# Other orders for the Strassen products of a two-layer encoder's MLP, with finer units of split weights

## The chip, the cores and the metric

One core of one Trainium2 chip runs the whole program. The metric is the device time of one execution in microseconds (us), the median of several runs. TensorE (PE in the profile) multiplies, VectorE (DVE), ScalarE (ACT) and GpSimd (POOL) do the element-wise work, SyncE (SP) issues the transfers; PSUM is the memory that TensorE accumulates in.

## The reference

An encoder of two layers on 544 tokens (512 of one sequence and 32 of another) of width 1024. Each layer adds two attention mixers, a cross-attention to 256 memory tokens and an MLP to the residual x. The change is in the MLP, and in what borders on it:

```
def rmsnorm(x, g):
    y = xf * lax.rsqrt(jnp.mean(jnp.square(xf), axis=-1, keepdims=True) + EPS)
    return y * g
...
    for l in range(DEPTH):
        x = x + mixers(rmsnorm(x, norm_mix[l]))
        x = x + cross_attention(rmsnorm(x, norm_cross[l]), mk, mv, w_xq[l], w_xo[l])
        hm = rmsnorm(x, norm_mlp[l])
        x = x + jnp.square(jax.nn.relu(hm @ w_up[l])) @ w_down[l]
    y = rmsnorm(x, norm_final)
```

Here w_up is 1024 x 4096 and w_down 4096 x 1024 in each layer, all in float32; the attention caches are outputs too.

## The kernel before

Activations lie transposed, features on the partitions, tokens along the free axis in two halves of 272. To keep float32's accuracy, each weight and activation is split into a high part (a cast by ScalarE to the short format fp32r) and a low part (a subtraction by VectorE, or by POOL in the attention), and a product is three matmuls: low x high, high x high, high x low (`mm3`).

The program is a list of steps with nominal costs (`then`), written in the order in which TensorE is to do them; a scheduler underneath may exchange neighbours that are ready. The order of each engine is fixed when the program is built, and an engine runs its own instructions strictly in that order.

The MLP (`mlp`, line 1405) goes through the 4096 hidden features in four groups per layer. A group has an *up stage*: eight blocks of 128 features (`dense`, 8 steps of 6 matmuls, 128x272 columns each, so 48), whose results `evac_up` brings out of PSUM, and from which `sums_up` and `rest_up` make the seven operands (B11, TA and so on) of a Strassen-Winograd scheme, again as high and low parts. Then comes the *down stage*: four *pairs* (two 128-feature blocks of the output each, `pair`, line 320). A pair loads its quarter of w_down with two transfers of 512 KB (L327), makes the weight sums S1 to S4 by four additions (`add`, L332), splits the seven weight operands in units (`split`, L342 on ScalarE and L343 on VectorE) and does seven products of 12 matmuls each (`product`, matmul on L358).

Three PSUM banks serve a pair: X and Z are the two halves of one tile (two such tiles exist, and the dense blocks use them too), W is another tile. The scheme's intermediate sums stay in the bank: after each product `evac_pair` (L1075, on VectorE) adds the bank as it then stands into one or two quarters of the residual X, and a later product goes on accumulating in the same bank. So the next product on a bank must wait until the addition after the one before has read it. `PRODUCTS` gives unit, operand and bank of the seven products; their banks in turn are X, Z, X, Z, X, W, X, pair after pair.

`UNITS` says which weight operands are split together: three units of two operands (1024 columns), which share a ring of two buffers (uh, ul), and one of one operand (512 columns), which takes a place in the ring of three (wh, wl) that the dense weights use as well. The table `todo` in `mlp` says before which product a load, an addition or a split is issued. In the last group of layer 0 each finished quarter is also prepared for the next layer's norm (`prep`: ScalarE's cast, VectorE's L401, ScalarE's square and POOL's sum L416), in the last of layer 1 for the final norm (`finish`, `final_sum`, `final_norm`), whose products by the norm's factor VectorE and POOL share by the table `OUT`. `next_block` says which dense weights are split during the last pair; `load_weights` issues their transfers (raw<-w_up, L238) on SP's queue, in which the transfers of w_down stand too.

## Time and profile before

| what | value |
|---|---|
| median of 3 runs | 1705.31 us (1704.8 to 1708.51) |
| profiled execution | 1705.88 us, span of its instructions 1704.1 us |
| mean granted TensorE clock | 0.993 of 2.4 GHz |
| TensorE busy | 1621.1 us, 12159 matmuls |
| VectorE busy | 1107.2 us |
| ScalarE busy | 794.6 us |
| POOL busy | 316.8 us |
| DMA | 157.22 MB, mean 92 GB/s |

The profile follows one execution. A row of a timeline gives the start and the duration of an instruction, engine, line, operation, the output and inputs by the program's names, and in brackets how long the engine had been idle and what it waited for. Matmuls overlap in the engine, so one is listed with 0.28 to 0.29 us although they start 0.12 to 0.13 us apart.

### The profile page before, as it was taken

The numbers are of one execution on the slowest core, as the hardware profiler recorded it, in microseconds if no ns is written. First come the engines' busy times: TensorE is split into PE (matmuls) and PEld (weight loads), VectorE is DVE, ScalarE is ACT, GpSimd is POOL, SyncE is SP. The second block draws the span as 40 slices with busy tenths as digits, with TensorE's granted clock in tenths as the row PEclk, the third lists the DMA queues.
The fourth block names the chain that finished last, engine by engine and source line by source line (L and its number), as shares of the span: only waits on it lengthen the run. The fifth ranks groups of instructions, "written<-read, shape, count | busy, mean of one in ns | idle before, by whom it ended". The sixth has DMA issues, their size and how long they took to land. (4 is left out here: it accounts for less than half of the span.)

```text
span 1704.1 us, 30118 instructions
## 1 busy us (share of the span) xinstructions
PE 1621.1 (95%) x12159; PEld 1516.3 (89%) x12159; DVE 1107.2 (65%) x2103; ACT 794.6 (47%) x1509; POOL 316.8 (19%) x297
## 2 busy tenths in 40 slices
PE   8899999999999999999889999999999999998995
PEld 7777889998999989899887778999999999898995
DVE  6956673456667677676777657535576676766765
ACT  6656664444443434334446646544444334243443
POOL 4514233321200000000244213333120000000003
PEclk9999999999999999999999999999999999999998
DMA  4322255223323222222123113642232222222211
GB/s 162 97 70 76 79 165 164 87 75 107 95 70 105 80 83 93 81 92 79 39 85 96 64 58 110 188 118 85 75 112 87 87 87 87 87 82 80 88 63 53
DMA packets 56395, 157.22 MB, mean 92 GB/s; under 512 B 6768, under 2 KB 16048, under 8 KB 56256
## 3 DMA queue, kind: packets, MB, share of 16 engines
q1 hardware_dynamic: 55984, 155.02, 29.2%
q8 instruction: 95, 1.56, 0.4%
q14 instruction: 44, 0.36, 0.1%
q10 hardware_dynamic: 272, 0.28, 0.0%
HBM read 143.49 MB, written 11.75 MB: 91 GB/s over the span
## 5 line engine op out<-in xcount | busy, mean ns | idle before, releaser
L289 PE MATMUL pd<-Ah,wl 128*128 128x272 f32 (+2 forms) x2032 | 458.9, 296 | 8.5 <-DVE wl L259 5.6
L289 PE MATMUL pd<-Ah,wh 128*128 128x272 f32 (+2 forms) x2032 | 441.5, 288 | 1.2 <-ACT Ah L400 1.2
L289 PE MATMUL pd<-Al,wh 128*128 128x272 f32 (+2 forms) x2032 | 440.4, 288 | 0.1
L256 ACT CAST wh<-raw 128x512 fp32r<-128x512 f32 (+1 forms) x362 | 222.0, 615 | 317.8 <-PE pd L289 244.7
L289 PEld LDWEIGHTS pd<-Ah,wl 128*128 128x128 f32 (+1 forms) x2032 | 327.9, 188 | 21.3 <-issue 9.6
L289 PEld LDWEIGHTS pd<-Ah,wh 128*128 128x128 f32 (+1 forms) x2032 | 327.1, 188 | 2.8 <-ACT Ah L400 2.2
L289 PEld LDWEIGHTS pd<-Al,wh 128*128 128x128 f32 (+1 forms) x2032 | 327.3, 188 | 0.3 <-DVE Al L401 0.3
L416 POOL TENSOR_TENSOR acc<-acc,sq 128x544 f32<-128x544 f32 x47 | 75.8, 1612 | 854.1 <-ACT sq L415 500.3
L259 DVE TENSOR_TENSOR wl<-raw,wh 128x512 fp32r<-128x512 f32 (+1 forms) x260 | 183.7, 707 | 50.8 <-ACT wh L256 50.3
L342 ACT CAST uh<-w 128x1024 fp32r<-128x1024 f32 x96 | 100.7, 1048 | 218.3 <-PE pd L358 214.9
L259 POOL TENSOR_TENSOR wl<-raw,wh 128x512 fp32r<-128x512 f32 (+1 forms) x102 | 133.0, 1304 | 338.0 <-ACT wh L256 229.6
L358 PE MATMUL pd<-Bh,ul 128*128 128x272 f32 x320 | 98.8, 309 | 38.6 <-DVE XG L1075 28.9
L1075 DVE TENSOR_TENSOR XG<-XG,pd 128x272 f32<-128x272 f32 x192 | 80.6, 434 | 78.5 <-PE pd L358 77.0
L343 DVE TENSOR_TENSOR ul<-w,uh 128x1024 fp32r<-128x1024 f32 x96 | 118.8, 1238 | 16.5 <-ACT uh L342 15.2
L289 PE MATMUL pd<-Bh,wl 128*128 128x272 f32 (+1 forms) x576 | 124.3, 294 | 1.2 <-DVE qr L718 0.7
L289 PE MATMUL pd<-Bh,wh 128*128 128x272 f32 (+1 forms) x576 | 121.2, 289 | 0.0
L289 PE MATMUL pd<-Bl,wh 128*128 128x272 f32 (+1 forms) x576 | 121.1, 289 | 0.0
L358 PEld LDWEIGHTS pd<-Bh,ul 128*128 128x128 f32 x320 | 60.6, 189 | 49.8 <-DVE XG L1075 34.5
L332 DVE TENSOR_TENSOR w<-w 128x512 f32<-128x512 f32 x128 | 92.4, 724 | 11.5 <-DMA w<-w_down 10.9
L289 PEld LDWEIGHTS pd<-Bh,wl 128*128 128x128 f32 x576 | 90.6, 188 | 3.8 <-issue 1.0
L358 PE MATMUL pd<-Th,ul 128*128 128x272 f32 x320 | 92.8, 290 | 0.0
L358 PE MATMUL pd<-Bl,uh 128*128 128x272 f32 x320 | 92.8, 290 | 0.0
(309 smaller groups left out, 3077.7 us busy)
## 6 DMA issues: line engine op xcount, KB each, us to landing
w<-w_down SPq DMA_DIRECT2D x64, 512.0 KB, 4.4
raw<-w_up SPq DMA_DIRECT2D x64, 512.0 KB, 3.5
raw<-w_in SPq DMA_DIRECT2D x28, 512.0 KB, 3.5
raw<-w_mk SPq DMA_DIRECT2D x16, 512.0 KB, 3.8
raw<-w_mv SPq DMA_DIRECT2D x16, 512.0 KB, 3.8
raw<-w_out SPq DMA_DIRECT2D x16, 512.0 KB, 3.6
raw<-w_xq SPq DMA_DIRECT2D x16, 512.0 KB, 3.6
raw<-w_xo SPq DMA_DIRECT2D x16, 512.0 KB, 3.6
```

The source lines that it names most:

```text
L256: nc.scalar.copy(h[:, :n], r)
L259: eng.tensor_tensor(lo[:, :n], r, h[:, :n].bitcast(F32), ALU.subtract)
L289: nc.tensor.matmul(o, w, a[:, c0:c1], start=start and n == 0, stop=stop and n == 2)
L332: self.nc.vector.tensor_tensor(w[:, o], w[:, a], w[:, b], ALU.add)
L342: self.nc.scalar.copy(h, r)
L343: self.nc.vector.tensor_tensor(lo, r, h.bitcast(F32), ALU.subtract)
L358: self.nc.tensor.matmul(st[bank], w[:, c], a, start=first and i == 0 and m == 0, stop=i == HP - 1 and m == 2, skip_group_check=True)
L416: nc.gpsimd.tensor_tensor(self.acc, self.acc, sq, ALU.add)
L1075: self.nc.vector.tensor_tensor(x, x, ps, op)
```

## The change

The seven products of a pair come in another sequence, with names (Q1, N5, N6, Q3, Q7, Q2, P4), and the table `GROUP` interleaves the pairs of a group (`LAST` does so for the last group of layer 1). W22 and W12 become units of their own, so that a pair has two units of 1024 and three of 512 columns. `plan` works out from `GROUP` and from the sizes of the two rings (`RINGS`) before which product a split, a load or an addition stands. All eight weight additions of a group's first two pairs move into its up stage (six before), and the first splits of pairs 0 and 1 too. The last product of a group, P4 of pair 3, runs inside the first block of the next group's up stage, after three of its eight steps (`resume`), with its split, its addition and the next load; for the last group of layer 0 that block is the first of layer 1. `AT` moves the norm and its use in layer 1's start, `final_norm` takes the rows of `OUT` by the order of the two halves, and the last sums of the final norm are made by halves for two pairs. Lines below the tables lie ten further down than before: 1075 becomes 1085, 358 becomes 368.

```diff
@@ -30,7 +30,7 @@
 
 AT = (dict(norm=1, take=(1.1, 2, 3), gate=3.5, sums=15, keys=24, rows=24, norm_cq=16, norm_ckv=22, split_ckv=27,
             rotary=25),
-      dict(norm=7, take=[13], gate=21, sums=42, keys=45, rows=51, norm_cq=38, norm_ckv=42, split_ckv=53, rotary=54))
+      dict(norm=10, take=[15], gate=21, sums=42, keys=45, rows=51, norm_cq=38, norm_ckv=42, split_ckv=53, rotary=54))
 
 POS = (dict(kr=1, v0=1, v1=4, qr0=2, qr1=2),
        dict(kr=1, v0=1, v1=3, qr0=2, qr1=2))
@@ -55,10 +55,20 @@
 W11, S1, W12, W22, S3, S2, S4 = range(7)
 W21 = S1
 
-UNITS = ((W11, 2), (S2, 2), (S3, 1), (W12, 2))
-
+UNITS = ((W11, 2), (S2, 2), (W12, 1), (S3, 1), (W22, 1))
+
+Q1, N5, N6, Q3, Q7, Q2, P4 = range(7)
 PRODUCTS = ((0, 0, B11, "X", True), (0, 1, TA, "Z", True), (1, 0, TB, "X", False), (1, 1, B22, "Z", False),
-            (2, 0, TC, "X", False), (3, 0, B21, "W", True), (3, 1, TD, "X", False))
+            (3, 0, TC, "X", False), (2, 0, B21, "W", True), (4, 0, TD, "X", False))
+
+GROUP = ((0, Q1), (0, N5), (1, Q1), (1, N5), (0, N6), (0, Q3), (0, Q2), (0, Q7), (1, N6), (1, Q3), (0, P4), (1, Q2),
+         (1, Q7), (2, Q1), (2, N5), (1, P4), (2, N6), (2, Q3), (2, Q2), (2, Q7), (3, Q1), (3, N5), (2, P4), (3, N6),
+         (3, Q3), (3, Q2), (3, Q7), (3, P4))
+
+LAST = GROUP[:18] + ((3, Q1), (2, Q7), (3, N5), (2, Q2), (3, N6), (3, Q3), (3, Q2), (3, Q7), (2, P4), (3, P4))
+
+RINGS = ((2, (0, 1), 4), (3, (2, 3, 4), 7))
+TAIL = 3
 HP = 4
 
 PAIRED = (0, 4, 1, 5, 2, 6, 3, 7)
@@ -1075,13 +1085,13 @@
         self.nc.vector.tensor_tensor(x, x, ps, op)
         if goff is None:
             return
-        if goff == G_FIN and i == HP - 1:
-            if n == 4:
+        if goff == G_FIN and i >= HP - 2:
+            if n == Q7:
                 self.finish(i, 1)
                 self.finish(m, 1)
-            elif n > 4:
+            elif n in (Q2, P4):
                 self.finish(m, 0)
-        elif n > 4:
+        elif n in (Q2, P4):
             if goff == G_FIN:
                 self.square(m)
                 self.nc.scalar.mul(self.X[:, m], self.X[:, m], self.g[:, goff + m:goff + m + 1])
@@ -1104,7 +1114,7 @@
         c = slice(j * HALF, (j + 1) * HALF)
         self.nc.tensor.matmul(ps, self.ones_r.bitcast(F32), self.acc[:, c], start=True, stop=False)
 
-    def final_norm(self, j):
+    def final_norm(self, j, n):
         nc = self.nc
         c = slice(j * HALF, (j + 1) * HALF)
         R = self.rp.tile([128, NT], F32, tag="r", name="R")
@@ -1112,7 +1122,7 @@
-        for b, eng in OUT[j]:
+        for b, eng in OUT[n]:
...
@@ -1293,12 +1303,13 @@
-            self.then([(0, lambda l=l: self.open_mixers(l))])
+            if l == 0:
+                self.then([(0, lambda: self.open_mixers(0))])
...
-            tkf = win(None, take[0], 96, **first)
+            tkf = win(None, take[0], 96, ahead=0)
...
@@ -1309,8 +1320,8 @@
                 first = [ckv] + f0
                 take = [lambda f=f, j=j: f(raw[j]) for j, f in enumerate(evac)]
             else:
-                first = [tkf] + cq + [ckv] + f0
                 take = [tkf.pop()[1]]
+                first = [self.resume(tkf, tail, len(self.order) - 7)] + cq + [ckv] + f0
             flat = [s for j in first for s in j]
             p = AT[l]
             assert p["norm"] <= p["take"][0] <= p["gate"] <= p["sums"] <= p["keys"] <= p["rows"]
@@ -1400,14 +1411,15 @@
                          for h in range(4)], t[3] + 8.4)
 
             goff = G_MIX + 8 if l == 0 else G_FIN
-            self.mlp(l, A, goff, bind, at, behind)
+            tail = self.mlp(l, A, goff, bind, at, behind)
 
     def mlp(self, l, A, goff, bind, at, behind):
         groups = []
         for grp in range(4):
-            up = [self.dense(io["w_up"][l, 8 * grp + j], 128, *A, bind(self.evac_up, j), ahead=int(n < 7))
-                  for n, j in enumerate(PAIRED)]
+            up = [self.dense(io["w_up"][l, 8 * grp + j], 128, *A, bind(self.evac_up, j),
+                             ahead=int(n < 7 and (n or not grp))) for n, j in enumerate(PAIRED)]
             down = [self.pair(io["w_down"][l, grp, i], lambda n, ps, i=i, g=goff if grp == 3 else None:
                               self.evac_pair(i, g, n, ps)) for i in range(HP)]
             groups.append((up, down))
@@ -1417,23 +1429,16 @@
         def do(f, *a):
             self.then([(0, lambda: f(*a))])
 
...
+        def call(n, what, *a):
             if n < len(pairs):
+                pairs[n][what](*a)
+
+        do(call, 0, "load")
+        do(call, 1, "load")
+        tail = None
         for grp, (up, down) in enumerate(groups):
             p0 = HP * grp
+            end = l == L - 1 and grp == 3
             if grp == 0:
                 up[0], up[1] = behind(up[0], up[1], self.norm, *NORM[l]["mlp"])
             for n in range(8):
@@ -1443,72 +1448,84 @@
                     up[n + 1] = at(up[n + 1], 5 + late, self.rest_up)
                     up[n + 1] = at(up[n + 1], 2 + late, self.sums_up, j)
 
-                if n >= 2:
-                    up[n] = at(up[n], 8, adds, p0 + (n >= 6), *((0, 1, 2, 3, 0, 1)[n - 2:n - 1]))
+                if n:
+                    up[n] = at(up[n], 8, call, p0 + n // 5, "add", (n - 1) % 4)
                 if n == 7:
-                    up[n] = at(up[n], 1, split, p0, 0)
-                    up[n] = at(up[n], 5, split, p0, 1)
+                    up[n] = at(up[n], 9, call, p0 + 1, "add", 3)
+                    up[n] = at(up[n], 1, call, p0, "split", 0)
+                    up[n] = at(up[n], 5, call, p0 + 1, "split", 0)
+            if grp:
+                up[0] = self.resume(up[0], tail, after - 8 * (4 - grp))
             for s in up:
                 self.then(s)
...
+            prods = LAST if end else GROUP
+            todo = self.plan(prods, p0, call)
+            q1 = len(prods) - (0 if end else 1)
+            todo[0].insert(0, (self.sums_up, 7))
+            todo[1].insert(0, (self.rest_up,))
+            if not end:
+                nxt = after - 8 * (3 - grp)
+
+                late = [(call, p0 + HP - 1, "split", 4), (call, p0 + HP + 1, "load")]
+                todo = {q: [f for f in fs if f not in late] for q, fs in todo.items()}
+                todo[q1 - 3].append((self.split_weights, nxt, 1))
+                todo[q1 - 1].extend(late)
             for q, (i, n) in enumerate(prods):
-                p = p0 + i
-                if q == 0:
-                    do(self.sums_up, 7)
-                if q == 1:
-                    do(self.rest_up)
-                for f, *a in todo.get((i, n), []):
+                for f, *a in todo.get(q, []):
                     do(f, *a)
-                if l == L - 1 and grp == 3 and q == len(prods) - 1:
-                    do(self.final_sum, 1)
-                self.then([(1.5, lambda p=p, n=n: pairs[p]["product"](n))])
-                if before:
-                    do(pairs[before[0]]["evac"], before[1])
-                before = p, n
-            do(pairs[before[0]]["evac"], before[1])
+                if q == q1:
+                    break
+                self.then([(1.5, lambda p=p0 + i, n=n: pairs[p]["product"](n))])
+                if q:
+                    i, n = prods[q - 1]
+                    do(pairs[p0 + i]["evac"], n)
+            i, n = prods[q1 - 1]
+            if end:
+                self.pn = {}
+                do(self.final_sum, 1)
+            do(pairs[p0 + i]["evac"], n)
+            tail = [(1.5, lambda p=p0 + HP - 1: pairs[p]["product"](P4))], [
+                (0, lambda p=p0 + HP - 1: pairs[p]["evac"](P4))]
         if l == L - 1:
-            self.pn = {}
-            do(self.final_norm, 1)
+            do(self.final_norm, 1, 0)
             do(self.final_sum, 0)
-            do(self.final_norm, 0)
-        do(self.close_mlp)
-
...
+    def resume(self, steps, tail, idx):
+
+        product, evac = tail
+        w = [[(0, lambda a=a: self.split_weights(*a))] for a in ((idx,), (idx + 1, 1), (idx + 1,))]
+        return (w[0] + steps[:TAIL] + product + steps[TAIL:TAIL + 1] + evac + steps[TAIL + 1:TAIL + 3] + w[1] +
+                steps[TAIL + 3:8] + w[2] + steps[8:])
+
+    def plan(self, prods, p0, call):
+
+        use, free, todo = {}, {}, {}
+        for q, (i, n) in enumerate(prods):
+            use.setdefault((i, PRODUCTS[n][0]), []).append(q)
+
+        def when(q, i, *a):
+            todo.setdefault(q, []).append((call, p0 + i) + a)
+
+        for rank, (ring, units, ahead) in enumerate(RINGS):
+            order = sorted((k for k in use if k[1] in units), key=lambda k: use[k][0])
+            for n, (i, u) in enumerate(order):
+                q = max(use[order[n - ring]][-1] + 1 if n >= ring else 0, use[i, u][0] - ahead)
+                assert q < use[i, u][0] or (i, u) == (0, 0)
+                free[i] = max(free.get(i, 0), q)
+                if u or i > 1:
+                    todo.setdefault(q + 0.5, []).append((call, p0 + i, "split", u))
+        for i in range(HP):
+            when(free[i] + 0.7, i + 2, "load")
+        for i in (2, 3):
+            a, b = [use[i, u][0] - 5 for u in (0, 1)]
+            for k, q in enumerate((a - 1, a, b - 1, b)):
+                when(max(q, free[i - 2] + 3), i, "add", k)
+        return {q: [f for k in sorted(todo) if int(k) == q for f in todo[k]] for q in range(len(prods))}
 
     def run(self):
         nc, io = self.nc, self.io
```

VectorE at the start of a group's down stage (the first of layer 0). L1131 and L1148 to L1154 bring out the last up block and form its sums, L1139 the low parts of the operands, L1075 adds a bank into the residual XG; pd_6060 is the tile with banks X and Z of pair 0, pw_6144 its bank W. Before:

```order
L1139 TENSOR_TENSOR Tl3_5109<-G_5110,Th3_5107 128x272
L1139 TENSOR_TENSOR Tl3_5109<-G_5110,Th3_5107 128x544 x2
L1075 TENSOR_TENSOR XG_85<-XG_85,pd_6060 128x272
L343 TENSOR_TENSOR ul_6094<-w_5501,uh_6093 128x1024
L1075 TENSOR_TENSOR XG_85<-XG_85,pd_6060 128x272 x2
L332 TENSOR_TENSOR w_6097<-w_6097 128x512
L343 TENSOR_TENSOR ul_6128<-w_5504,uh_6127 128x1024
L1075 TENSOR_TENSOR XG_85<-XG_85,pd_6060 128x272 x2
L1075 TENSOR_TENSOR XG_85<-XG_85,pw_6144 128x272
```

In the changed kernel (ten lines further down), pd_6070 is the tile of pair 0 and pd_6102 that of pair 1:

```order
L1149 TENSOR_TENSOR Tl3_5109<-G_5110,Th3_5107 128x272
L1149 TENSOR_TENSOR Tl3_5109<-G_5110,Th3_5107 128x544 x2
L1085 TENSOR_TENSOR XG_85<-XG_85,pd_6070 128x272
L353 TENSOR_TENSOR ul_6099<-w_5501,uh_6098 128x1024
L1085 TENSOR_TENSOR XG_85<-XG_85,pd_6070 128x272
L1085 TENSOR_TENSOR XG_85<-XG_85,pd_6102 128x272 x2
L353 TENSOR_TENSOR ul_6137<-w_5504,uh_6136 128x1024
L342 TENSOR_TENSOR w_6120<-w_6120 128x512
L1085 TENSOR_TENSOR XG_85<-XG_85,pd_6070 128x272 x2
L1085 TENSOR_TENSOR XG_85<-XG_85,pw_6166 128x272
```

After the first two additions of pair 0 come two of pair 1, and only then the third and fourth of pair 0; the split in front of them is of pair 1's weights.

TensorE where a group ends and the next up stage begins; pd_6407 and pd_6414 hold banks X and Z of pair 3, pd_6522 and pd_6525 are the first up block's. Before, the last product stood in front of most of the block (single steps were pulled ahead of it):

```order
L289 MATMUL pd_6522<-Al_87,wh_6458 128x272 x2
L289 MATMUL pd_6522<-Ah_86,wl_6459 128x272 x2
L289 MATMUL pd_6522<-Ah_86,wh_6458 128x272 x2
L358 MATMUL pd_6407<-Bh_88,ul_6439 128x272
L358 MATMUL pd_6407<-Bh_88,uh_6438 128x272
L358 MATMUL pd_6407<-Bl_89,uh_6438 128x272
L358 MATMUL pd_6407<-Bh_88,ul_6439 128x272
```

In the changed kernel, where 18 matmuls of the block stand ahead of it:

```order
L299 MATMUL pd_6525<-Ah_86,wl_6468 128x272 x2
L299 MATMUL pd_6525<-Ah_86,wh_6467 128x272 x2
L299 MATMUL pd_6525<-Al_87,wh_6467 128x272 x2
L368 MATMUL pd_6414<-Bh_88,wl_6499 128x272
L368 MATMUL pd_6414<-Bh_88,wh_6498 128x272
L368 MATMUL pd_6414<-Bl_89,wh_6498 128x272
```

The last product of the group now has 18 matmuls between it and the product before it on the same tile, and takes its weights from a 512-column unit (wl_6499) instead of a half of a 1024-column one (ul_6439).

SP's queue from the first to the second group of layer 0, with the transfers of w_down for the next pairs and of the next up blocks' weights. Before:

```order
L327 DMA w_6097<-w_down 128x1024 x2
L327 DMA w_6212<-w_down 128x1024 x2
L327 DMA w_6328<-w_down 128x1024 x2
L238 DMA raw_6492<-w_up 128x1024
L327 DMA w_6442<-w_down 128x1024 x2
L238 DMA raw_6555<-w_up 128x1024
```

In the changed kernel:

```order
L337 DMA w_6120<-w_down 128x1024 x2
L337 DMA w_6252<-w_down 128x1024 x2
L337 DMA w_6344<-w_down 128x1024 x2
L337 DMA w_6502<-w_down 128x1024 x2
L248 DMA raw_6523<-w_up 128x1024
L248 DMA raw_6595<-w_up 128x1024
```

The raw weights of the third up block now stand behind both later transfers of w_down.

## Rows read from the trace of the kernel before

**Rows 1.** The page's span and busy times.
```profile
span 1704.1 us, 30118 instructions
...
PE 1621.1 (95%) x12159; PEld 1516.3 (89%) x12159; DVE 1107.2 (65%) x2103; ACT 794.6 (47%) x1509; POOL 316.8 (19%) x297
```

**Rows 2.** Windows by stage, from:to, width, each engine's busy time (instructions), clock, DMA share, GB/s.
```profile
600.00:650.79 50.79, 46.92 (x354) 44.75 (x353) 37.95 (x64) 16.84 (x20) 0.00 (x0) 1.00 0.29 94
650.79:697.20 46.41, 46.41 (x370) 46.41 (x369) 30.41 (x47) 21.23 (x30) 0.00 (x0) 1.00 0.26 80
...
794.63:849.50 54.87, 47.69 (x344) 44.97 (x342) 39.92 (x62) 22.81 (x31) 8.57 (x5) 0.97 0.16 50
...
1436.87:1490.76 53.89, 48.44 (x355) 46.23 (x353) 38.12 (x64) 16.83 (x20) 0.00 (x0) 0.97 0.26 88
...
1537.16:1589.53 52.37, 46.97 (x355) 44.79 (x354) 37.96 (x64) 16.82 (x20) 0.00 (x0) 1.00 0.28 91
...
1635.93:1688.90 52.97, 46.17 (x342) 43.43 (x341) 34.20 (x55) 23.67 (x33) 9.91 (x7) 1.00 0.12 40
sum 695.64, PE 655.43 PEld 636.86 DVE 484.49 ACT 274.81 POOL 18.48; mean PE 46.82 PEld 45.49 DVE 34.61 ACT 19.63 POOL 1.32
```

**Rows 3.** The page's costliest groups: products, splits and adds of w_down, and dense matmuls.
```profile
L289 PE MATMUL pd<-Ah,wl 128*128 128x272 f32 (+2 forms) x2032 | 458.9, 296 | 8.5 <-DVE wl L259 5.6
...
L358 PE MATMUL pd<-Bh,ul 128*128 128x272 f32 x320 | 98.8, 309 | 38.6 <-DVE XG L1075 28.9
...
L343 DVE TENSOR_TENSOR ul<-w,uh 128x1024 fp32r<-128x1024 f32 x96 | 118.8, 1238 | 16.5 <-ACT uh L342 15.2
...
L332 DVE TENSOR_TENSOR w<-w 128x512 f32<-128x512 f32 x128 | 92.4, 724 | 11.5 <-DMA w<-w_down 10.9
```

**Rows 4.** TensorE's timeline around the third product of the group from 600.00.
```profile
604.83 0.39 PE L358 MATMUL pd<-Bh,ul 128*128 128x272 f32 x1 [1.66 <-DVE XG L1075]
...
606.29 0.29 PE L358 MATMUL pd<-Tl,uh 128*128 128x272 f32 x1
```

**Rows 5.** VectorE's timeline at the same place.
```profile
602.72 1.71 DVE L1139 TENSOR_TENSOR Tl<-G,Th 128x272 fp32r<-128x272 f32 x3
604.34 0.43 DVE L1075 TENSOR_TENSOR XG<-XG,pd 128x272 f32<-128x272 f32 x1
604.69 1.22 DVE L343 TENSOR_TENSOR ul<-w,uh 128x1024 fp32r<-128x1024 f32 x1
606.62 0.44 DVE L1075 TENSOR_TENSOR XG<-XG,pd 128x272 f32<-128x272 f32 x1 [0.71 <-PE pd L358]
...
609.73 0.69 DVE L332 TENSOR_TENSOR w<-w 128x512 f32<-128x512 f32 x1 [0.38 <-DMA w<-w_down]
```

**Rows 6.** VectorE's timeline, two late w_down loads.
```profile
1460.98 0.69 DVE L332 TENSOR_TENSOR w<-w 128x512 f32<-128x512 f32 x1 [2.40 <-DMA w<-w_down]
...
1548.51 0.69 DVE L332 TENSOR_TENSOR w<-w 128x512 f32<-128x512 f32 x1 [1.99 <-DMA w<-w_down]
```

**Rows 7.** The page's DMA issues, KB each, median us to landing.
```profile
w<-w_down SPq DMA_DIRECT2D x64, 512.0 KB, 4.4
```

**Rows 8.** The window behind the first of those loads.
```profile
1465.00:1470.00 5.00, 4.47 (x28) 4.25 (x27) 3.63 (x7) 1.85 (x2) 0.00 (x0) 0.79 0.00 0
```

**Rows 9.** VectorE's timeline in the last group of layer 0.
```profile
822.00 0.78 DVE L401 SCALAR_TENSOR_TENSOR Al<-XG,Ah 128x544 fp32r<-128x544 f32 x1
...
825.62 1.85 DVE L401 SCALAR_TENSOR_TENSOR Al<-XG,Ah 128x544 fp32r<-128x544 f32 x1
827.39 0.43 DVE L1075 TENSOR_TENSOR XG<-XG,pd 128x272 f32<-128x272 f32 x1
```

**Rows 10.** TensorE's timeline at the start of layer 1.
```profile
881.59 0.53 PE L289 MATMUL pd<-Ah,wl 128*128 128x272 f32 x2 [2.77 <-POOL wl L259]
```

**Rows 11.** TensorE's timeline before the last product of all.
```profile
1687.55 0.73 PE L1105 MATMUL pf<-acc,ones_r 128*128 128x272 f32 x2 [0.85 <-POOL acc L416]
```

**Rows 12.** POOL's timeline in the final norm.
```profile
1696.63 3.69 POOL L1120 TENSOR_TENSOR XG<-XG,R 128x272 f32<-128x272 f32 x4 [2.26 <-DVE R L393]
```

More of the change, by code (lines that the diff above doesn't have):

```diff
@@ L1123, in final_norm @@
                     nc.vector.scalar_tensor_tensor(x, x, g, R[:, :HALF], ALU.mult, ALU.mult)
-            (nc.scalar if eng and j else nc.sync).dma_start(out=o[:, b, c], in_=self.X[:, b, c])
+            (nc.scalar if eng and n else nc.sync).dma_start(out=o[:, b, c], in_=self.X[:, b, c])
     def evac_up(self, j, ps):
@@ L1418, in do @@
             self.then([(0, lambda: f(*a))])
-        def ready(n):
+        def call(n, what, *a):
             if n < len(pairs):
-                pairs[n]["load"]()
-        def adds(n, *which):
-            if n < len(pairs):
-                for a in which:
-                    pairs[n]["add"](a)
-        def split(n, u):
-            if n < len(pairs):
-                pairs[n]["split"](u)
-        do(ready, 0)
-        do(ready, 1)
+                pairs[n][what](*a)
+        do(call, 0, "load")
+        do(call, 1, "load")
+        tail = None
         for grp, (up, down) in enumerate(groups):
             p0 = HP * grp
+            end = l == L - 1 and grp == 3
             if grp == 0:
@@ L1471, in mlp @@
-            nxt = self.next_block(l, grp, after)
-            if nxt is not None:
-                when(HP - 1, 3, self.split_weights, nxt, 1)
-                when(HP - 1, 5, self.split_weights, nxt)
-            else:
-                prods[14:] = prods[14:19] + prods[21:26] + prods[19:21] + prods[26:]
-                p = p0 + 2
-                todo[2, 2] = [(split, p + 1, 0)]
-                todo[2, 4] = [(adds, p + 1, 3)]
-                todo.pop((2, 5))
-                todo[3, 2] = [(split, p, 3)]
-                todo[3, 4] = [(split, p + 1, 3)]
```

25 lines of the change are left out of this document (5 added, 20 removed).

## The prediction

> **What bounds the kernel now.** The page's first lines come first: TensorE is busy for 95% of the span and no other engine for more than 65% [rows 1], so time can only be won where TensorE stands still or runs slower, and the work left on it sets the floor. The windows by stage come second [rows 2]. In an up stage (the row from 650.79, one of six alike) 46.41 us hold 370 matmuls and TensorE is busy to the last hundredth: 46.41/370 = 0.1254 us for one matmul of 272 columns when nothing is late. A group is 8 up blocks of 48 matmuls and 28 products of 12, so 384 + 336 = 720 matmuls, 90.3 us at that pace. The group from 600.00 takes 50.79 + 46.41 = 97.2 us: 6.9 us too long, all of it in the down stage. The same sum gives 10.0 for the group from 1436.87 and 8.5 for that from 1537.16; the last groups of the layers, whose windows hold 342 matmuls (42.9 us), are 12.0 (from 794.63) and 10.1 us (from 1635.93) too long. The sum row has all 14 windows: 695.6 us against 5004 matmuls or 627.7 us, so 68 us in excess, and the three plain groups not shown hold the 20.6 that are left, 6.9 each.
>
> Third, the costliest groups name the waits [rows 3]: the first matmul of a product stands 28.9 us behind DVE's addition of the bank into the residual (L1075), most of its 38.6; DVE itself waits 10.9 us for w_down (L332). The dense matmuls wait only 8.5 us in the whole kernel. Fourth, the timelines show how such a stall comes about. The third product of the group, which goes on in the bank of the first, starts at 604.83 after 1.66 us of idling [rows 4], because the addition of the first product stood in DVE's queue behind the 1.71 us of L1139 and ran at 604.34 [rows 5].
>
> What one re-use needs comes from the same rows: the last matmul of a product starts at 606.29, its addition starts at 606.62 and takes 0.44, and TensorE starts 0.06 after such an addition ends (604.34 + 0.43 = 604.77, then 604.83). That is 0.83 us. Now one product, 12 x 0.1254 = 1.5 us, lies between two uses of a bank, so DVE has 0.7 us of slack, less than one split of 1024 columns (1.24 us, [rows 3]). Every split or add that is under way, and every add that waits for its weights, shows through.
>
> **The change, part by part.** *New order of products.* By the order of the instructions, 18 to 36 matmuls of other banks now lie between two uses of one bank, 2.25 to 4.5 us, so the slack is 1.4 to 3.7 us: a 1.24 us split fits, and at most places a split and an add. I walked the new DVE order through one group with the durations of [rows 3, 5], the first product at T = 0. The first addition runs at 4.34 as now, the S2 split ends at 5.9, the third use of the first pair's tile is due at 6.25: the 1.66 us stall goes, with 0.3 us to spare. The next load goes out when that split has freed its weights, as now (604.69 + 1.22 = 605.91, and the first add starts at 609.73, 3.8 us later, [rows 5]), so its first add can start at 9.7, and the addition queued behind it ends at 10.75, when Q7 of pair 0 is due: 0.1 us of stall. The load after that gives 23.8 against 24.0: just met. All other gaps hold. The first splits of the next up stage come 0.1 to 0.15 us late. I take 1.0 us of excess for each of the six plain groups in place of the present 6.9 (four times), 10.0 and 8.5.
>
> *Slow loads.* Twice the add waited 2.40 and 1.99 us [rows 6] where that at 609.73 waited 0.38 [rows 5], so those loads came 1.6 to 2.0 us later (the median landing is 4.4 us, [rows 7]). These are the groups with 10.0 and 8.5. After the first of them the granted clock was 0.79 of full speed [rows 8], between the two levels of 1.2 and 2.4 GHz, so its price was more than the wait. In the new order a load late by 1.6 us moves the addition behind it by 1.6 and meets 0.1 us of slack: 1.5 us. With two such loads again: 3 us in all (4 by the later one).
>
> *Finer units.* One split of 1024 per pair becomes two of 512: on DVE 2 x 0.69 (the width of the adds: 0.72 on average [rows 3], 0.69 at 609.73 [rows 5]) for 1.24, about 0.15 us more, 16 pairs in a layer. The unit also sits in the ring of three with the dense weights. The work is hidden as long as DVE has room. It has 37.95 us of work in the 50.79 of a down stage; by the walk 35.4 of 44.2 remain, since two adds, two splits and one product's split and addition go to the up stage (30.4 of 46.4 now [rows 2]). That is 80% in the place of 75%; what it costs if a queue forms is rival 1.
>
> *Product P4 of pair 3 in the next up block.* Its 12 matmuls run after 18 of the dense ones, and the product's W22 split gets that much more time; nothing is added or removed. The second up block needs the tile of pair 3, 30 matmuls (3.8 us) after P4's end, against 0.83: no wait. The w_down load issued there now stands ahead of both next w_up loads on SP; it is bounded below: zero if the raw tiles come in time, and at most 0.15 per group, which is in the 1.0.
>
> *Last groups.* In layer 0 the preparation of the next norm has eight operations of 0.78 us (L401) on DVE, and beside POOL's sums some take longer: 1.85 us at 825.62, and the addition behind it came at 827.39 [rows 9]. In the walk one such delay (about 1.8) reaches TensorE at P4 of pair 1, and I leave 3.5 us of the 12.0; in layer 1, with half-width sums at the end, 2.0 of the 10.1.
>
> The Trainium skill, page "SBUF — State Buffer", section "Who interferes with whom", says that a VectorE instruction with two SBUF inputs and a GpSimd instruction that reads SBUF exclude each other, the later one waiting for the whole of the earlier. The 1.85 for 0.78 agrees with a wait for the rest of a POOL sum, not for all of it. If instead each of the five POOL sums of this group met a DVE operation at its start, by an estimate from that page each could cost its whole length; the sum would then leave this group where it is now, some 1660.
>
> *Start of layer 1.* The earlier norm and the change of its slots may remove two waits on the norm's sums, but TensorE then waits 2.77 us at 881.59 for POOL's split [rows 10], at the end of a chain that begins with the last addition of layer 0 and that the change does not shorten. What is won before is waited for there. Bounds -0.75 to +0.5, taken as 0.
>
> *Tail.* TensorE's last wait of 0.85 us [rows 11] is in the excess already. The second half of the final norm now gives POOL two products instead of four (3.69 us for four [rows 12]) and DVE the others; the gain lies between 0 and 1 us; I take 0.5.
>
> **The sum.** Left over: 6 x 1.0 + 3 + 3.5 + 2.0 = 14.5 of 68, so 53.5 us less, and 0.5 at the tail: 54.0. The profiled execution took 1705.88 us (span 1704.1 and 1.8 around it), 0.57 more than the median of 1705.31. From it, 1705.9 - 54.0 = 1651.9: I forecast 1652 us. If all the excess went, it would be 1705.9 - 68 - 0.5 = 1637.
>
> **The rivals.**
> 1. *DVE's queue becomes the bound.* Additions now stand behind adds that wait for w_down; the walk meets two places per group by 0.1 to 0.2 us. If loads come 1.6 us later as a rule, both cost 1.5 in each of six plain groups, 18 us, less the 3 already counted: 1667; with the last groups and some clock lost as at [rows 8], up to 1680. For it: the median landing of 4.4 is longer than the 3.8 that I used, by 0.6. Against it: only two waits of about 2 us among all groups. Chance 0.22.
> 2. *The last groups keep their excess*, POOL and DVE holding each other up there: 8.5 + 8 more, 1660 to 1668. For it: [rows 9]; against it: slack of 1.4 us and more takes in one delay of 1.07. Chance 0.10.
> 3. *Everything is hidden*: 1637 to 1643. Against it are the margins of 0.1 us in the walk. Chance 0.06.
> 4. *The order does not hold*: the order in which DVE adds the banks shows it does in the program, but if the waits are really for the splits, they stay and the time stays near 1705. Only part of the waits [rows 3] is DVE's split's. Chance 0.03.
> 5. *Slower: the w_up loads come late.* Place: the first up blocks of a group, where both raw loads now stand behind two w_down transfers on SP's queue. Price: each microsecond late stops TensorE for one in a stage that has no stall now. It turns the gain round from 9 us per group on, in the six groups with a next one (6 x 9 = 54); at 10 us it would be 6 us slower, 1711. Against it: a landing of 4.4 us, and 48 matmuls (6 us) of cover. Chance 0.03.
>
> **How the numbers follow.** My forecast (1645 to 1658) has 0.56, the rivals 0.22, 0.10, 0.06, 0.03 and 0.03 in turn. The low end, 1643, leaves out most of rival 3; the high end, 1676, takes in rival 2 and most of rival 1, as well as late loads in most groups; about 0.15 is left out. Faster by over 0.2% (3.4 us, about what measuring this kernel can tell from no change): 0.94; within 0.2%: 0.03, rival 4; slower by over 0.2%: 0.03, rival 5.
>
> **What would show it.** Right: down stages of about 44 to 46 us with TensorE full; the wait of products on L1075 (now line 1085) a few us instead of 28.9; no stall at the third use of a group's first bank; the up stages still 46.4 plus 1.5 for the carried product; the last group of layer 0 near 46. Rival 1 would show as waits of 1 to 2 us on line 1085 at Q7 of pair 0 and N6 of pair 2, each just after a DVE wait for w_down; rival 2 as DVE splits of 2 us beside POOL's sums; rival 5 as waits of dense matmuls on wl in the first up blocks, with the split waiting for w_up. The forecast is wrong if the plain groups still take over 94 us.

## The result and the profile after

The changed kernel takes 1653.86 us in the median (four runs, 1651.53 to 1655.14), the kernel before 1705.05: a ratio of 0.9695, 95% interval 0.9677 to 0.9712, so 51 us less. Forecast were 1652 us in 1643 to 1676. The sum came out; what it was put down to did not, as the experiments show.

The page of the changed kernel: TensorE's share is up from 95 to 97% [rows 1], VectorE's from 65 to 67.

```profile
PE 1602.4 (97%) x12159; PEld 1512.4 (92%) x12159; DVE 1110.5 (67%) x2135; ACT 800.2 (48%) x1545; POOL 313.5 (19%) x299
...
L342 DVE TENSOR_TENSOR w<-w 128x512 f32<-128x512 f32 x128 | 93.2, 730 | 35.7 <-DMA w<-w_down 35.2
L352 ACT CAST uh<-w 128x1024 fp32r<-128x1024 f32 x64 | 67.2, 1051 | 79.3 <-DVE w L342 60.9
...
L353 DVE TENSOR_TENSOR ul<-w,uh 128x1024 fp32r<-128x1024 f32 x64 | 78.1, 1220 | 2.4 <-ACT uh L352 2.4
```

VectorE now waits 35.2 us for w_down in the place of 10.9 [rows 3], and TensorE hardly notices. The group of a product's first matmuls, with its 38.6 us of idling, is no longer among the costliest. TensorE's waits for the residual's additions, once 28.9 us, are down to 5.7; the view of waits gives total, times and longest:

```profile
PE pd L977 <- DVE Kn L963: 7.1, 4, 2.6
PE pd L368 <- DVE XG L1085: 5.7, 12, 1.1
...
PE pd L299 <- POOL wl L269: 4.0, 3, 3.1
```

The windows by stage, columns as in [rows 2]: a down stage, its up stage, the last group of layer 0, a down stage of layer 1 and the last one.

```profile
594.37:639.55 45.18, 44.91 (x355) 44.34 (x354) 36.96 (x65) 16.82 (x23) 0.00 (x0) 1.00 0.27 88
639.55:685.23 45.68, 45.68 (x369) 45.68 (x368) 31.38 (x49) 21.79 (x31) 0.00 (x0) 1.00 0.32 99
...
776.02:824.95 48.93, 45.99 (x358) 44.74 (x357) 42.96 (x68) 24.17 (x37) 8.86 (x6) 1.00 0.13 45
...
1500.28:1546.19 45.91, 45.08 (x355) 44.37 (x354) 37.12 (x65) 16.88 (x23) 0.00 (x0) 1.00 0.25 86
1591.87:1637.20 45.33, 43.31 (x339) 42.38 (x338) 35.52 (x58) 24.70 (x41) 9.91 (x9) 1.00 0.14 47
```

The group shown takes 45.18 + 45.68 = 90.86 us against 97.2, where 720 matmuls need 90.3. VectorE's timeline at its start, the place of [rows 5], follows the walk of the prediction closely (594.37 is its T = 0):

```profile
597.09 1.71 DVE L1149 TENSOR_TENSOR Tl<-G,Th 128x272 fp32r<-128x272 f32 x3
598.71 0.43 DVE L1085 TENSOR_TENSOR XG<-XG,pd 128x272 f32<-128x272 f32 x1
...
604.15 0.69 DVE L342 TENSOR_TENSOR w<-w 128x512 f32<-128x512 f32 x1 [1.29 <-DMA w<-w_down]
604.75 0.90 DVE L1085 TENSOR_TENSOR XG<-XG,pd 128x272 f32<-128x272 f32 x2
```

The first addition runs at T = 4.34, as before, and no product waits for it. The add that waits for its load runs at T = 9.78 (walked: 9.7), and the one stall of the group is at Q7 of pair 0, 0.27 us where 0.1 was walked (it ends with the second of the two additions behind the add, at 605.65; the walk had Q7 wait for the first):

```profile
605.71 0.39 PE L368 MATMUL pd<-Bh,wl 128*128 128x272 f32 x1 [0.27 <-DVE XG L1085]
...
800.25 0.40 PE L368 MATMUL pw<-Bh,wl 128*128 128x272 f32 x1 [0.91 <-DVE wl L353]
801.89 0.40 PE L368 MATMUL pd<-Bh,wl 128*128 128x272 f32 x1 [1.12 <-DVE XG L1085]
...
854.41 0.53 PE L299 MATMUL pd<-Ah,wl 128*128 128x272 f32 x2 [3.05 <-POOL wl L269]
...
885.27 0.38 PE L977 MATMUL pd<-wh,Bl 128*128 128x256 f32 x1 [2.20 <-DVE Kn L963]
888.75 0.69 PE L474 MATMUL pt<-ident,P 128*128 128x128 f32 x2 [2.02 <-DVE P L459]
```

The next two rows are the last group of layer 0, the last three the start of layer 1. There something got worse: from the last product of layer 0 to the first of layer 1 it took 488.76 us before (851.01 to 1339.77) and now 494.25 (824.65 to 1318.90). Behind the waits of 3.05, 2.20 and 2.02 us the granted clock was 0.66 of full speed in the mean of 5 us, between its levels of 1.2 and 2.4 GHz:

```profile
855.00:860.00 5.00, 5.00 (x26) 4.69 (x25) 1.51 (x3) 1.64 (x3) 0.60 (x1) 0.66 0.59 185
885.00:890.00 5.00, 2.70 (x15) 2.31 (x16) 5.00 (x13) 3.30 (x10) 4.22 (x4) 0.66 0.09 16
```

After the wait of 2.77 us in the same place before [rows 10], the next 5 us ran at 1.00.

The rows of the whole stretch, the kernel before and then the changed one, show what was lost:

```profile
851.01:1339.77 488.76, 476.18 (x3555) 434.67 (x3554) 299.91 (x647) 250.39 (x555) 139.12 (x128) 1.00 0.32 97
824.65:1318.90 494.25, 480.50 (x3555) 440.25 (x3554) 300.33 (x646) 250.61 (x554) 134.56 (x127) 0.98 0.32 97
```

The matmuls are the same in number. Of the 5.5 us TensorE is idle for 1.2 (13.75 less 12.58); the other 4.3 are its own busy time, at a lower mean clock (0.98 against 1.00). Part of that has no new wait in front of it. TensorE waits 1.32 us up to 951.40 and 1.43 up to 1033.37, and in the same places of the kernel before 1.32 up to 973.85 and 1.45 up to 1055.03. Behind these waits the changed kernel (first two rows) was granted 1.2 GHz, the kernel before 2.4:

```profile
951.50:954.50 3.00, 3.00 (x14) 3.00 (x15) 2.34 (x11) 1.47 (x6) 1.27 (x1) 0.50 0.02 7
1033.50:1036.50 3.00, 3.00 (x15) 3.00 (x16) 2.97 (x12) 1.04 (x4) 0.00 (x0) 0.50 0.68 195
...
973.95:976.95 3.00, 3.00 (x24) 2.74 (x24) 2.90 (x11) 2.46 (x10) 1.29 (x1) 1.00 0.02 7
1055.15:1058.15 3.00, 3.00 (x26) 3.00 (x27) 2.97 (x12) 1.79 (x5) 0.64 (x1) 1.00 0.65 193
```

### The profile page after: what moved, and what is told of

It reads as the page before. It is cut to its first block, busy times and chain, and to the rows that moved or that the text cites. A ratio compares the mean times of both kernels' runs of the same rounds, so it can differ in the third digit from the quotient of the medians.

```text
span 1652.3 us, 30168 instructions
## 1 busy us (share of the span) xinstructions
PE 1602.4 (97%) x12159; PEld 1512.4 (92%) x12159; DVE 1110.5 (67%) x2135; ACT 800.2 (48%) x1545; POOL 313.5 (19%) x299
## 4 chain that ended last, share of the span: by engine, by line
PE 79%; DVE 10%; DMA 4%; ACT 2%; POOL 1%; issue 1%; DVEq 0%; SPq 0%; POOLq 0%; ACTq 0%
PE pd L299 53%; PE pd L368 11%; DMA w<-w_down 2%; PE pw L368 2%; PE pt L474 1%; PE S L641 1%; PE S L573 1%; PE pv L668 1%; PE pv L527 1%; DVE XG L1085 1%; DVE ul L353 1%; PE S L572 1%; PE pv L587 1%; PE S L509 1%; DVE w L342 1%; PE pd L977 1%
## 5 line engine op out<-in xcount | busy, mean ns | idle before, releaser
L426 POOL TENSOR_TENSOR acc<-acc,sq 128x544 f32<-128x544 f32 x45 | 69.2, 1538 | 806.7 <-ACT sq L425 806.5
L352 ACT CAST wh<-w 128x512 fp32r<-128x512 f32 x96 | 59.5, 619 | 142.1 <-PE pw L368 62.0
L342 DVE TENSOR_TENSOR w<-w 128x512 f32<-128x512 f32 x128 | 93.2, 730 | 35.7 <-DMA w<-w_down 35.2
L352 ACT CAST uh<-w 128x1024 fp32r<-128x1024 f32 x64 | 67.2, 1051 | 79.3 <-DVE w L342 60.9
L299 PEld LDWEIGHTS pd<-Bl,wh 128*128 128x128 f32 x576 | 91.1, 189 | 0.3
L299 PEld LDWEIGHTS pd<-Bh,wh 128*128 128x128 f32 x576 | 90.6, 188 | 0.5
L353 DVE TENSOR_TENSOR ul<-w,uh 128x1024 fp32r<-128x1024 f32 x64 | 78.1, 1220 | 2.4 <-ACT uh L352 2.4
L1141 DVE SCALAR_TENSOR_TENSOR up<-pd,R 128x544 f32<-128x544 f32 x64 | 46.2, 722 | 45.7 <-PE pd L299 45.7
```

The costliest lines, as they stand in the source:

```text
L299: nc.tensor.matmul(o, w, a[:, c0:c1], start=start and n == 0, stop=stop and n == 2)
L342: self.nc.vector.tensor_tensor(w[:, o], w[:, a], w[:, b], ALU.add)
L352: self.nc.scalar.copy(h, r)
L353: self.nc.vector.tensor_tensor(lo, r, h.bitcast(F32), ALU.subtract)
L426: nc.gpsimd.tensor_tensor(self.acc, self.acc, sq, ALU.add)
L1141: nc.vector.scalar_tensor_tensor(halves(t), ps[:, :, :HALF], 0.0, halves(self.R), ALU.max, ALU.mult)
```

## The experiments

Each is an edit of the changed kernel. Beside the medians the profiled executions are compared by stretches, since the time to the first product alone varied from 500.6 to 506.9 us among kernels that are alike up to there.

**Order and units, two by two.** *Old order, new units:*

```diff
-GROUP = ((0, Q1), (0, N5), (1, Q1), (1, N5), (0, N6), ...
+GROUP = tuple((i, n) for i in range(4) for n in range(7))
...
-                    up[n] = at(up[n], 5, call, p0 + 1, "split", 0)
+                    up[n] = at(up[n], 5, call, p0, "split", 1)
...
```

> The products pair after pair again (banks X, Z, X, Z, X, W, X), with the new units, rings and carried last product. Theory (the distance between two uses of a bank carries the gain): most stalls of products on the additions come back, down stages of 47 to 50 us instead of 45.1, 1675 to 1700 us in all. Rival (the finer units, the adds moved into the up stage or the carried product carry it): 1653 to 1662 us.

1660.59 us, ratio 0.9745 (0.9730 to 0.9759): the old order costs 7 us, not 20 to 45. The theory fell and the rival held.

*New order, old units* (in the last group of layer 1 the products stand as in the others, and there the addition after Q7 of pair 3 reads its bank after P4):

```diff
-UNITS = ((W11, 2), (S2, 2), (W12, 1), (S3, 1), (W22, 1))
+UNITS = ((W11, 2), (S2, 2), (S3, 1), (W12, 2))
...
-RINGS = ((2, (0, 1), 4), (3, (2, 3, 4), 7))
+RINGS = ((2, (0, 1, 3), 4), (3, (2,), 7))
```

> The new order with the units of before (three of 1024 columns on a ring of two, one of 512), the last group in the same order as the others. Theory (the new order needs the finer units): at two or three places of a group the split can start only when P4 of the pair before has freed its buffer, 1.05 us cast and 1.24 us subtraction with 1.5 us of other work to cover it; 1 to 2.5 us each, 1665 to 1700 us in all. Rival (the order alone does it): 1650 to 1658 us.

1701.22 us, ratio 0.9976 (0.9963 to 0.9989), just above the theory's range: the new order by itself gains some 4 us of the 51. Its waits for splits of the unit of W12 are what the theory named (total, times, longest), and waits for additions stand beside them:

```profile
PE pd L368 <- DVE XG L1085: 20.9, 18, 2.7
PE pw L368 <- DVE ul L353: 17.8, 16, 2.0
```

*Both old*, the two edits together, with everything else of the change left in:

> Old order and old units, with the rest of the change left in (the planned places of splits and loads, eight additions in the up stage, the carried last product). Completes a table of two by two with the first batch (old order with new units 1660.6, new order with old units 1701.2, both new 1653.9). Theory that the finer units carry the gain: 1690 to 1705 us. Rival, that the planned places, the moved additions or the carried product do: 1660 to 1680 us.

1704.9 us, ratio 1.0003 (0.9989 to 1.0018). So planned places, moved additions and carried product give nothing by themselves in the sum. In the profiled executions they do something: from first to last product the two MLPs take 690.3 us together, in the kernel before 696.7; but layer 1's attention takes 495.4 instead of 488.8, of which 5.3 us are TensorE's busy time for the same matmuls (481.51 and 476.18), the clock again. The table by medians: both old 1704.9, order alone 1701.2, units alone 1660.6, both 1653.9. The units give 44 us with the old order and 47 with the new, the order 4 and 7. The two MLPs alone, whose mean granted clock is 1.00 in all of them, say the same: 690.3 both old, 686.0 order alone, 646.1 units alone, 639.2 both.

How they do it is seen at the first re-use of a bank in a group. With both old TensorE waits as in [rows 4]:

```profile
602.99 0.40 PE L366 MATMUL pd<-Bh,ul 128*128 128x272 f32 x1 [1.67 <-DVE XG L1083]
```

With the old order and the new units, at the same place:

```profile
597.81 0.29 PE L366 MATMUL pw<-Tl,wh 128*128 128x272 f32 x1
598.26 0.40 PE L366 MATMUL pd<-Bh,ul 128*128 128x272 f32 x1 [0.16 <-DVE XG L1083]
```

and on VectorE beside it:

```profile
596.15 1.71 DVE L1147 TENSOR_TENSOR Tl<-G,Th 128x272 fp32r<-128x272 f32 x3
597.78 0.43 DVE L1083 TENSOR_TENSOR XG<-XG,pd 128x272 f32<-128x272 f32 x1
```

The 1.71 us and the addition behind it are the same as before; but TensorE has done a whole product on bank W (pw, 12 matmuls up to 597.81) meanwhile. The scheduler drew Q2 ahead, and could, since W12, now a unit of its own on the ring of three, was split during the up stage. The distance between two uses of a bank is what counts, as predicted; the finer units make it, and the written order adds little.

**Small splits or free buffers?** W12 and W22 are split apart, but take their buffers from the ring of two, in the old order:

```diff
-            if n == 1:
+            if u in (2, 4):
+                h, lo = [self.mlp_pool.tile([128, 2, 512], F32R, tag="u" + x, name="u" + x, bufs=2)[:, :1] for x in "hl"]
+            elif n == 1:
...
-RINGS = ((2, (0, 1), 4), (3, (2, 3, 4), 7))
+RINGS = ((2, (0, 1, 2, 4), 4), (3, (3,), 7))
```

> Old order and the new units, but W12 and W22 (512 columns each) take their buffers from the ring of two of the 1024-column units instead of the ring of three. Tells apart why finer units help. Theory A (what counts is that the ring of two has two users per pair instead of three, so that splits can be made ahead and operands lie ready): no better than the old units, 1695 to 1720 us. Theory B (what counts is that one split holds VectorE for 0.69 instead of 1.24 us): 1655 to 1670 us, as with the old order and the new units on their own rings (1660.6).

1727.64 us, ratio 1.0153 (1.0137 to 1.0169): slower than the kernel before, and above the range of either theory. Short splits are worth nothing if their buffers come late; TensorE waits 48.5 us for the additions here. The other half, the old units on a ring with a third buffer, was not tried. The line of ScalarE's casts into the shared ring, for five kernels: before; old order on the crowded ring; both old; new order with old units; old order with new units.

```profile
L342 ACT CAST uh<-w 128x1024 fp32r<-128x1024 f32 x96 | 100.7, 1048 | 218.3 <-PE pd L358 214.9
```
```profile
L352 ACT CAST uh<-w 128x1024 fp32r<-128x1024 f32 (+1 forms) x128 | 106.6, 833 | 230.1 <-PE pd L368 199.1
```
```profile
L350 ACT CAST uh<-w 128x1024 fp32r<-128x1024 f32 x96 | 100.6, 1048 | 216.6 <-PE pd L366 213.2
```
```profile
L352 ACT CAST uh<-w 128x1024 fp32r<-128x1024 f32 x96 | 100.6, 1049 | 181.9 <-PE pd L368 174.3
```
```profile
L350 ACT CAST uh<-w 128x1024 fp32r<-128x1024 f32 x64 | 67.1, 1049 | 93.5 <-PE pd L366 89.2
```

ScalarE idles before these casts until a product has freed a buffer: 215 us before, then 199, 213, 174, 89, and 16 in the changed kernel, whose row above waits for the weights instead. The sum of this idling is no measure of the loss: the slowest kernel does not have the most, and before the casts into the ring of three (wh) all idling rises from 27.8 us before to 142.1 in the changed kernel, where products wait 0.9 us in all for such a split. Taken together ScalarE idled 246 us before and 221 now. What differs is which operand can be made ahead, as that of Q2 above.

**The load.** *Each load issued one product later:*

```diff
-            when(free[i] + 0.7, i + 2, "load")
+            when(free[i] + 1.7, i + 2, "load")
```

> Each w_down load of the down stage is issued one product (1.5 us) later. Theory (the adds that wait for it stand ahead of additions with 0.1 to 0.2 us of slack): up to 1.5 us more at two places of each group, 15 to 25 us in all, 1668 to 1680 us. Rival (the queue has room, the walk's margins were too narrow): 1652 to 1658 us.

1652.68 us, ratio 0.9708 (0.9685 to 0.9731): no difference, and no test. SP waits in its queue for the buffer, and issues at T = 5.93 in both kernels (600.30 - 594.37, and 597.23 - 591.30). It serves as a second run of the changed kernel: its attention in layer 1 took 490.98 us, so some 3 of the 5.5 us lost there vary between executions. Most of them are the clock's: TensorE idles for 13.34 us, nearly as in the changed kernel (13.75), but is busy for 477.64 instead of 480.50. *The first half transferred twice:*

```diff
-            for c, o in ((0, W11), (1, W12)):
+            for c, o in ((0, W11), (0, W11), (1, W12)):
```

> The first half of each quarter of w_down is transferred twice, one after the other, so the additions of weights can start some 1.5 us later (issuing the load one product later had moved nothing, since SP's queue waits for the buffer anyway). Theory of the prediction's first rival (additions into the residual stand behind the waiting ones with 0.1 to 0.2 us of slack): about 1.4 us at two places of each plain group, 1668 to 1685 us. Rival (the queue has room): 1653 to 1660 us.

1665.67 us, ratio 0.9760 (0.9744 to 0.9776): between the two. A plain group takes 92.15 to 92.56 us in layer 0, 1.6 more. The price is paid at one place, and not where the theory had it: the scheduler, which builds VectorE's order anew for each kernel, put the additions ahead of the waiting adds, and it is a split of the next pair's weights that comes late. So this is not the price of late loads in the order of the changed kernel, which no run shows:

```profile
630.08 0.39 PE L368 MATMUL pd<-Bh,ul 128*128 128x272 f32 x1 [1.56 <-DVE ul L353]
```

**The carried product.** In both kernels here the norm and its use in layer 1 stand one step earlier (`AT`). In the first one P4 of pair 3 stays right behind Q7; the addition between them then reads its bank after P4, so that its wait is missing too, and the time is only a lower bound.

```diff
-            q1 = len(prods) - (0 if end else 1)
+            q1 = len(prods)
...
-                todo[q1 - 1].extend(late)
...
-            tail = [(1.5, lambda p=p0 + HP - 1: pairs[p]["product"](P4))], [
-                (0, lambda p=p0 + HP - 1: pairs[p]["evac"](P4))]
+            tail = [], []
```

> The last product of a group stays at the end of its down stage, right after Q7 on the same bank. Theory: each of the seven such places waits for one addition with nothing in between, 0.83 us and what stands in VectorE's queue, 0.9 to 1.5 us each, 6 to 10 us in all: 1659 to 1664 us. Rival (the scheduler's freedom and the next block hide it, or the carrying costs layer 1's start as much as it saves): 1649 to 1656 us.

1646.04 us, ratio 0.9661 (0.9637 to 0.9685). With Q2 between Q7 and P4 (`(3, Q7), (3, Q2), (3, P4)` at the end of `GROUP`) it counts in full:

> The last product stays in its down stage, now with Q2 between Q7 and P4 of pair 3, so that every addition reads its bank before the next product on it (in the earlier run without carrying, one addition per group came a product late, and its wait was missing). Theory A (carrying the last product costs as much at layer 1's start as it saves): the stretch from layer 0's last product to layer 1's first takes 490 us instead of 494, groups 0.3 to 1 us longer each; 1648 to 1654 us in all. Theory B (the carrying saves a wait in each group): 1658 to 1664 us.

1658.35 us, ratio 0.9719 (0.9702 to 0.9736), against 0.9695 with the carrying; the intervals overlap. Both theories hold in part. Groups take 91.82 to 93.93 us in the place of 90.64 to 91.59, so carrying pays within a layer. The stretch between the layers is shorter: 489.64 us from last to first product, 490.40 in the first kernel, with the carrying 490.98 (load late) to 494.25. Without the carrying it even holds 18 matmuls more (2.3 us), which otherwise stand ahead of the carried product. But TensorE's busy time in it, 478.50 us for 3573 matmuls, is about 476.2 without these 18, as in the kernel before, against 477.64 and 480.50: 1.4 to 4.3 us of what seems the carrying's cost are the clock's, the rest waits (idle for 11.14 us, with the carrying 13.34 and 13.75). The next kernel carries too and takes 486.87, so it is not shown that carrying must cost anything there. A kernel that carries only within the layers was not tried.

**The start of layer 1 and the last group of layer 0.** The low half of one block's weights moves from POOL to VectorE, and the rotary key's transfers from SP to ScalarE:

```diff
-        eng = nc.gpsimd if j % 2 and i > 2 and not self.in_mlp else nc.vector
+        eng = nc.gpsimd if j % 2 and i > 2 and i not in self.on_dve and not self.in_mlp else nc.vector
...
-        nc.sync.dma_start(out=self.io["o_kr"][l], in_=kr[0:64])
+        q = nc.scalar if l else nc.sync
+        q.dma_start(out=self.io["o_kr"][l], in_=kr[0:64])
```

> In layer 1's start, the low half of the fox-k weights is made by VectorE instead of POOL, and the three small transfers of the rotary key are issued by ScalarE instead of SP. Theory (the 5.5 us that layer 1's attention lost hang on TensorE's wait of 3.05 us for POOL's split and on two waits of 2 us behind the late sine table): 3 to 6 us less than the changed kernel, 1648 to 1651 us. Rival (the chain from the last addition of layer 0 sets the time, and a wait taken away comes back behind it): 1652 to 1656 us.

1646.07 us, ratio 0.9654 (0.9640 to 0.9669): faster than the change, by some 7 us, more than the theory's 3 to 6. The attention of layer 1 takes 486.87 us:

```profile
827.49:1314.36 486.87, 476.25 (x3555) 435.37 (x3554) 298.47 (x647) 250.57 (x554) 133.72 (x126) 1.00 0.32 99
```

Against the changed kernel 3.1 of the 7.4 us are waits and 4.3 busy time at a lower clock. The mean granted clock of its four runs is 0.992 to 0.995, of the changed kernel's 0.987 to 0.990. Each part alone:

> One of the two parts of the earlier combination (1646.1): only the low half of the fox-k weights made by VectorE instead of POOL. If the wait of 3.05 us for POOL's split carries the loss of layer 1's start: 1648 to 1650 us. If the late sine table does: 1652 to 1655 us.

> The other part alone: the rotary key's three small transfers issued by ScalarE, so that SP's queue is free for the sine and cosine tables. If the late tables carry the loss: 1648 to 1650 us. If the wait for POOL's split does: 1652 to 1655 us.

Ratios 0.9693 (0.9675 to 0.9711; 1650.4 us) and 0.9690 (0.9668 to 0.9711; 1648.74 us), beside a kernel before of 1702.62 in that session: against the change's 0.9695, neither alone can be told from it; the stretches are 489.98 and 492.05 us. Each part takes about 1.9 us from TensorE's idle time there (11.91 and 11.78 in the place of 13.75). The busy time is 478.07 and 480.27, within the 477.64 to 480.50 of the kernel with late loads and the changed one, whose waits are alike, so these profiles do not say how much of the clock's share hangs on either wait.

Last, the sums of squares of layer 0's last group on VectorE too:

```diff
-            nc.gpsimd.tensor_tensor(self.acc, self.acc, sq, ALU.add)
+            (nc.vector if dve else nc.gpsimd).tensor_tensor(self.acc, self.acc, sq, ALU.add)
```

> The combination (1646.1), and the seven sums of squares in layer 0's last group made by VectorE instead of POOL. Theory (a POOL sum holds a VectorE operation that starts beside it for about 1.1 us, and with it the additions): some 2 us of the 3.5 that this group takes longer than the others go, 1643 to 1645 us. Rival (seven more operations of 0.72 us on VectorE cost what the undisturbed ones gain): 1645 to 1648 us.

1643.68 us, the lowest median of all, ratio 0.9660 (0.9645 to 0.9675), not distinguishable from 0.9654. In its profile the group does what was expected: its products span 46.56 us instead of 48.99. On VectorE a norm preparation now takes 0.78 us (at 794.73) and the sum behind it 0.72.

## Why the prediction was right, and where it was not

The spans fell by 1704.1 - 1652.3 = 51.8 us, and the stretches add up to it: 97.01 + 97.20 + 97.43 - 90.83 - 90.86 - 90.79 = 19.2 in the first three groups, 7.8 in the last of layer 0 (products' span 56.38 to 48.63), 23.2 in three groups of layer 1, 7.5 in the last, 0.2 at the tail; less 5.5 for layer 1's attention and 0.6 before the first product.

- **The kernel before** was read rightly: stalls behind L1075 at re-used banks, 6.9 us per plain group.
- **What is left over per plain group** was walked as 1.0 us and measured as 0.3 to 0.6, once 1.3 (91.59 - 90.3). The walk's times for VectorE were right to 0.1 or 0.2 us because it went by the order of the instructions as built, which already held what units and scheduler had made of the table.
- **"New order of products"**, the step to which the 1.66 us stall and the rest were credited, failed as an attribution. The order is worth 4 us alone and 7 beside the units. With the old units it gave what rival 4 foresaw, waits for splits (17.8 us) and a time near the old one.
- **"Finer units"**, costed at 0.15 us on VectorE and hidden, was the term that carried 44 to 47 us. The prediction looked at the length of a split; what changed was the ring that it waits for. The 214.9 us that ScalarE's casts waited for products before stood on the page and were not used: three users share two buffers, so that a unit like that of W12, the operand of Q2, could not be split ahead. VectorE itself idled 15.2 us for these casts [rows 3], now 2.4, and the additions behind in its queue with it; how much of the 44 us that makes is not shown.
- **"Slow loads"**, 3 us, did not come. VectorE waited three times as long for w_down, and products waited for additions for 5.7 us in all. One plain group, from 1500.28, took 91.59 us, 0.8 to 1.0 more than the others. Rival 1 did not come. The doubled transfer costs 1.6 us per group, but in another order of VectorE, so its price stays unknown.
- **"Last groups"** was right within a microsecond: in layer 0, 48.93 us for 358 matmuls (44.9) leaves 4.0 (3.5 forecast); in layer 1, 45.33 less 42.9 is 2.4 (2.0). The Trainium skill's page "SBUF — State Buffer", section "Who interferes with whom", has it that a VectorE instruction with two SBUF inputs contends with a GpSimd instruction that reads SBUF, for ports that are locked exclusively. The trace agrees better than the prediction allowed: what the later one waits for is the end of the running sum. POOL's and VectorE's timelines of the combined kernel:

```profile
799.09 1.59 POOL L427 TENSOR_TENSOR acc<-acc,sq 128x544 f32<-128x544 f32 x1 [337.23 <-ACT sq L426]
800.87 1.61 POOL L427 TENSOR_TENSOR acc<-acc,sq 128x544 f32<-128x544 f32 x1 [0.18 <-ACT sq L426]
```
```profile
799.38 1.89 DVE L412 SCALAR_TENSOR_TENSOR Al<-XG,Ah 128x544 fp32r<-128x544 f32 x1
801.19 1.84 DVE L354 TENSOR_TENSOR wl<-w,wh 128x512 fp32r<-128x512 f32 x1
```

  POOL's sums end at 800.68 and 802.48, VectorE's operations that began beside them 0.59 and 0.55 later, a little less than they last alone (0.78 and 0.69). The four others in the MLPs of this kernel that began during such a sum, 0.01 to 0.62 us after its start, end 0.55 to 0.58 behind it. Rival 2 (all the excess kept) still did not come, as the slack took in most of it; with the sums on VectorE the group lost another 2.4 us.
- **"Start of layer 1"** was wrong: 0, bounded by -0.75 and +0.5, and measured +5.5 (2.2 in the second run of like code). That what is won before is waited for there was right (2.77 became 3.05 us), but two new waits of 2 us were not in it, and above all not the clock: 1.2 us of the 5.5 are idle time, 4.3 the same matmuls at a lower granted clock, in part behind waits that were there before.
- **"Tail"**: 0.25 us, 0.5 forecast. **Rival 5** (late w_up loads) did not come: 45.68 us for 369 matmuls is 0.124 each, no stall.

The sum was hit partly by luck. Over and under cancelled: 3 us too many were set down for loads and 2.4 for what is left in the plain groups, against 5.5 too few for layer 1's start and 2.2 for the last groups, the tail and the time to the first product.

## What to carry to other kernels

Where operands are made ahead on a ring, ask which buffer the next one waits for before asking how long it takes to make, and which product could run now if its operand were there. A written order may matter little under a scheduler that moves what is ready: give it ready work, and look at the order that comes out. And a forecast that is right in sum says nothing about its terms; a table of two by two of the parts costs two or three runs and would have put 44 us where they belong. Before a stretch's time is put down to a wait, compare TensorE's busy time for the same matmuls: here most of a loss was the clock's.

## What had not been expected of the hardware

The length of a wait does not say whether the granted clock falls behind it. At the same place of the program, TensorE's wait for POOL's split at the start of layer 1, the next 5 us were granted 0.66 after 3.05 us in the changed kernel and 1.00 after 2.77 before. But they were granted 1.00 after 2.98 us in the kernel with late loads and 0.66 after 2.75 in the second kernel without carrying:

```profile
851.70:856.70 5.00, 5.00 (x35) 4.80 (x36) 1.81 (x4) 1.76 (x4) 1.15 (x1) 1.00 0.58 186
```
```profile
858.00:863.00 5.00, 5.00 (x24) 4.77 (x25) 0.00 (x0) 1.19 (x3) 1.14 (x1) 0.66 0.54 184
```

What decides it stays open here. The price is seen in the matmuls done: 24 in these 5 us instead of 35.

And the same program text reached its first product between 500.6 and 506.9 us after the start, a spread as large as the order's whole effect, for which the stretches had to be compared. Between these two executions TensorE's busy time up to there differs by 3.9 us (484.71 and 488.56) for the same matmuls, so more than half of the spread is the clock's too.
